# Spread modulation, eight plain blocks, and low parts of weights added by a GpSimd-queue DMA

## The chip, the core and the metric

The kernel runs on one core of a Trainium2 chip. A core has engines that each work through their own instructions in order: TensorE (PE; its weight loads are listed as PEld), VectorE (DVE), ScalarE (ACT), GpSimd (POOL) and SyncE (SP), which here only issues DMAs. Sixteen DMA engines move data between HBM and the on-chip SBUF; the queues of SP, ACT and POOL feed the same sixteen. The metric is the device time of one execution in microseconds (us), as the median of several runs.

## The reference

Two layers of a diffusion transformer over 256 latent tokens and 256 context tokens, model width 1024, float32. Layer 0 mixes with a short convolution, layer 1 with attention (8 query heads, 2 key/value heads, width 128). Around each mixer stand two feed-forward networks (FFNs). Cut to what matters here:

```python
for i in range(DEPTH):                                   # 2
    mod  = (silu(c) @ mod_w[i] + mod_b[i])               # 9 vectors of 1024: shift, scale, gate x 3
    modc = (silu(c_ctx) @ mod_w[i] + mod_b[i])
    lat = lat + 0.5 * gate * swiglu(modulate(lat, norm_g, shift, scale), w13, w2)
    cx  = cx  + 0.5 * gate * swiglu(modulate(cx, ...), w13, w2)
    lat, cx = mixer(...)                                 # conv in layer 0, attention in layer 1
    lat = lat + 0.5 * gate * swiglu(...)                 # second FFN; cx too in layer 0
# swiglu(h) = (silu(h @ w_gate) * (h @ w_up)) @ w2, hidden width 2816 = 22 blocks of 128
# modulate(t) = rms_norm(t) * g * (1 + scale) + shift
```

## The kernel before

Activations lie transposed: 128 features on the partitions, 512 tokens in the free dimension (256 latent, then 256 context), in 8 such tiles. Matmuls run in the fp32r type, and to keep float32 accuracy each operand is split in a high part (`hi`, rounded to fp32r by a ScalarE copy) and a low part (`lo = x - hi`, by VectorE): `split` (L89 to L92). `mm3` (L111 to L117) then issues three matmuls per product: high by high (L115), high weights by low activations (L116), low weights by high activations (L117).

Weights come in 1 MB tiles on the SP queue (`load_raw`, L85 to L87; tag `wr`, three buffers) and are split by half tiles of 128 x 1024 (tags `wh` and `wl`, four buffers each).

An FFN (`ffn`, l and b for layer and place) works in thirds of 8, 7 and 7 hidden blocks. Each third first makes its hidden blocks from `w13`, then `project` multiplies them by its part of `w2` into the 8 output tiles (`py`), and `finish` (L417) adds them to the residual `x` with the gate.

A hidden block over 512 tokens is made in one of two ways. The plain way (`w13_mm`, `w13_post`) takes 8 x 2 x 3 = 48 matmuls of 512 columns. The `Pair` way multiplies the 2 x 2 block matrix of gate and up weights with the 2 x 2 block matrix of the two token halves by a scheme with seven products in place of eight: 7 x 4 x 3 = 84 matmuls of 256 columns. It needs sums of the weights (S1 to S4, made by VectorE at L519, L525, L527 and then split) and sums of the activations (T1 to T4, made once per FFN by `sums`). The blocks A11, A12 and A22 are raw weights: A11 and A12 share one half tile of 128 x 1024 (`wh`, `wl`), A22 has its own of 128 x 512 (`w4h`, `w4l`, two buffers). In TensorE's order a Pair begins with its head, A11 into `p` and A12 into `q` (24 matmuls), then S1; the previous Pair's S3; S2 and S4; the previous Pair's A22. All FFNs but the last, which has 256 tokens, use Pairs; FFN (0,0) has three plain blocks at its start, FFNs (0,1) and (1,0) one, in the middle of which two Pairs' heads are issued.

Modulation is done by VectorE beside the matmuls: `mod_job` loads 1 MB of transposed `mod_w` and reduces 128 rows of 1024 at a time against silu(c) (L138), two row tiles by two streams, so four reductions in a row. `tick(share)` is called after an output tile, a convolution tile and so on, and starts a job when the shares add up to one; `mod_ready` runs whatever is still owed at once when a scale, shift or gate is needed. All of it is done before the attention.

The order on each engine is made when the kernel is built: a planner goes through the program by priority and readiness, gives each tile a free buffer of its tag, and writes the waits. An instruction that writes into a reused buffer waits for that buffer's last reader.

`Blocks.block` (L268 to L285) makes the normalised activations for Pairs: ScalarE writes them in float32, and for the first block a split follows after every second tile of 256 columns.

Of the kernel before, what the change touches and what calls it, by code (L numbers as in the profile page):

```python
# [9 lines left out]
F32 = mybir.dt.float32  # L10
# [6 lines left out]
P = 128  # L17
# [3 lines left out]
T2 = 2 * S  # L21
NM = 22
THIRDS = (8, 7, 7)
HEADS = 8
KVH = 2
EPS = 1e-6
# [11 lines left out]
def hybrid_kernel(ctx: ExitStack, tc: tile.TileContext, a: dict, out: bass.AP):  # L38
# [9 lines left out]
    modctx = ExitStack()  # L48
    mp = modctx.enter_context(tc.tile_pool(name="mp", bufs=2))

    uid = [0]

    def nm(s):
        uid[0] += 1
        return f"{s}{uid[0]}"
# [34 lines left out]
    def split(hi, lo, src):  # L90
        nc.scalar.activation(out=hi, in_=src, func=AF.Copy)  # L91
        nc.vector.tensor_tensor(out=lo, in0=src, in1=hi.bitcast(F32), op=ALU.subtract)  # L92
# [30 lines left out]
    def mod_tile(l, ch):  # L123
# [2 lines left out]
            done[l, ch] = 0  # L126
        return modv[l, ch]

    def mod_job(l, ch, pair):
        mt = mod_tile(l, ch)  # L130
        nv = 1 if (l == 1 and ch >= 5) else 2
        raw = load_raw(a["modT"][l, ch * 4 + pair])
        for j in range(2):
            kt = pair * 2 + j
            col = ch * KT + kt
            for v in range(nv):
                junk = mp.tile([P, D], BF16, name=nm("junk"), tag="junk", bufs=1)
                nc.vector.tensor_tensor_reduce(  # L138
                    out=junk,
                    in0=raw[:, j * D : j * D + D],  # L140
                    in1=scbc[:, v, :],
                    scale=1.0,
                    scalar=modb[:, l, col : col + 1],
                    op0=ALU.mult,
                    op1=ALU.add,
                    accum_out=mt[:, kt, v : v + 1],
                )
        done[l, ch] += 1

    jobs = [(0, ch, p) for ch in range(2, 9) for p in range(4)]  # L150
    jobs += [(1, ch, p) for ch in range(9) for p in range(4)]
    owed = [0.0]

    def tick(share):

        owed[0] += share
        while jobs and owed[0] >= 1:
            owed[0] -= 1
            mod_job(*jobs.pop(0))

    def mod_ready(l, ch):
        while not ((l, ch) in done and done[l, ch] == 4):
            mod_job(*jobs.pop(0))
        return modv[l, ch]

    def scale_of(l, j):
# [98 lines left out]
    class Blocks:  # L265
# [5 lines left out]
        def block(self, s, hf, A, B, ri, fine=False):  # L271
            raw = self.raw[hf, s] = hot("hr", F32)
            hi, lo = self.t["B", hf, s] = hot("bh"), hot("bl")
            for i in range(4):
                k = 4 * hf + i
                c = slice(i * S, i * S + S)
                t = scaled(s, k, A, ri)
                nc.scalar.activation(
                    out=raw[:, c], in_=t, func=AF.Identity, bias=B[:, k, s : s + 1]
                )  # L280
                if fine and i % 2:
                    c = slice((i - 1) * S, (i + 1) * S)
                    split(hi[:, c], lo[:, c], raw[:, c])
            if not fine:
                split(hi, lo, raw)  # L285

# [146 lines left out]
    def project(ws, src, nk, gate, tail, tot, late, ev, between=()):  # L433

        def products(ps, w, ks, c0, c1):  # L440
            for k in ks:
                mm3(ps[:, : c1 - c0], w(k), src(k, c0, c1), k == 0, k == nk - 1)

        nf = 3 if between else 2
        w2 = [ws(m) for m in range(nf)]
        p2 = [psum("py") for _ in range(nf)]
        cut = nk - 2 if between else nk - 1
        for i in range(nf):
            products(p2[i], w2[i], range(cut), 0, tot)
            if i < len(between):  # L450
                between[i]()
        if between:
            for i in range(nf):
                products(p2[i], w2[i], (nk - 2,), 0, tot)
        for i in range(nf):
            products(p2[i], w2[i], (nk - 1,), 0, tot)
            finish(i, p2[i], 0, tot, gate, tail)
            tick(ev)

        for m in range(nf, KT - late):  # L460
            if tail and tot == S and m == KT - 2:
                ready()
            w = ws(m)
            ps = psum("py")
            products(ps, w, range(nk), 0, tot)
            finish(m, ps, 0, tot, gate, tail)
            tick(ev)
        if late:

            wl = [ws(m) for m in (6, 7)]  # L470
# [25 lines left out]
    class Pair:  # L496
# [6 lines left out]
        def __init__(self, src, h):  # L503
# [5 lines left out]
            s1, s2, s3, s4 = (sm[:, i * T2 : i * T2 + T2] for i in range(4))  # L509
            self.w = {}  # L510

            def keep(keys, src):
                hi, lo = half()
                split(hi, lo, src)
# [56 lines left out]
    def ffn(l, b, h, tot, gate, tail, gs=(), ev=0.5):  # L571
        gs = list(gs)
        i0 = 0
        for t, n in enumerate(THIRDS):
            between = ()
            if tot == T2:
# [12 lines left out]
                    w13_post(pp, gs[0], 0, T2)  # L589
                prev = None  # L590
                for i in range(len(gs), n):
                    if heads:
# [14 lines left out]
                    gs.append(new_pair("g"))  # L607
                    prev.four(gs[-1])

                between = (prev.seven, last)  # L610
            else:
                for i in range(n):
                    w = load_w(a["w13"][l, b, i0 + i])
                    gs.append(new_pair("g"))
                    pp = psum("pg"), psum("pu")
                    w13_mm(pp, w, h, range(KT), 0, tot)
                    w13_post(pp, gs[i], 0, tot)
            i0 += n
            box = {}

# [122 lines left out]
    }  # L743
    for step in FIRST_STEPS.split():
        steps[step[0]](*(int(c) for c in step[1:]))
    done[0, 0] = done[0, 1] = 4
    h = FirstBlocks(h, h32)
    h.sums()
    for i in range(3):
        gs0.append(new_pair("g"))  # L750
        w13_post(pps[i], gs0[i], 0, T2)
# [13 lines left out]
    for m in range(KT):  # L765
# [36 lines left out]
        tick(1.2)  # L802

    def by_pairs(key):
        box = {}
# [9 lines left out]
    hn = Blocks()  # L815
    project(
        by_pairs("cw_out"), lambda k, c0, c1: (zs[k][0][:, c0:c1], zs[k][1][:, c0:c1]), KT,
        lazy_gate(0, 1), tail_norm(0, 2, hn), T2, 2, 0.5,
    )
    h = hn  # L820
    hn = Blocks()
    ffn(0, 1, h, T2, lazy_gate(0, 2), tail_norm(1, 0, hn), ())
    h = hn


    hn = Plain()
    ffn(1, 0, h, T2, lazy_gate(1, 0), tail_norm(1, 1, hn), (), 0.9)
    h = hn
    mod_ready(1, 8)
    modctx.close()  # L830
    ap = ctx.enter_context(tc.tile_pool(name="ap", bufs=2))


# [8 lines left out]
                start=True, stop=True,  # L842
            )

    def rotate(ps, gain, n, tag):

        kn = ap.tile([P, T2], F32, name=nm("kn"), tag=tag)
# [27 lines left out]

    def q_rope(p, ps):
        sums(ps, 4 * p)
        qr = rotate(ps, qg, 2, "qn")
        qs.append(new_pair("q"))
        split(qs[p][0], qs[p][1], qr)  # L880

# [5 lines left out]

    def k_rope(kv, ps):
        sums(ps, 16 + 4 * kv)
        krs.append(rotate(ps, kg, 1, "kn"))  # L890

    vs = []
    vt = []
# [42 lines left out]
    q_rope(0, pq[0])  # L936
    wk = load_w(a["wk"])
    pk = [k_proj(0)]
    q_rope(1, pq[1])
    pk.append(k_proj(1))  # L940
    k_rope(0, pk[0])
    pq.append(q_proj(2))
    k_rope(1, pk[1])
    inv_rms(16, 24)
    pq.append(q_proj(3))
# [75 lines left out]
    for hd in range(HEADS):  # L1021
        if hd + 2 < HEADS:
            pns[hd + 2] = scores(hd + 2)
        pts[hd] = turn(pns.pop(hd))
        if hd:
            mix(hd - 1, pts.pop(hd - 1))
    mix(HEADS - 1, pts.pop(HEADS - 1))


    hn = Plain(S)  # L1030
    project(
        by_pairs("wo"), lambda k, c0, c1: aos[k], KT, lazy_gate(1, 1), tail_norm(1, 2, hn), S, 0, 0,
    )
    ffn(
        1, 1, hn, S, lazy_gate(1, 2),
# [81 lines left out]
```

## Time and profile before

| | |
|---|---|
| median of 3 runs | 1635.89 us (1634.96 to 1641.69) |
| profiled execution | 1636.17 us, its span 1634.1 us, granted TensorE clock 0.984 |
| busy PE, DVE, ACT, POOL | 1581.4, 1358.5, 735.1, 0.2 us |
| DMA | 248.81 MB, 152 GB/s in the mean |

How rows are read. A group of instructions: line, engine, operation, out<-in by the program's names, shape, xcount | busy us, mean ns of one | idle time before them and what ended it. A wait: who <- whom, then us in total, times, longest us. A row in order of time: start in us from the span's beginning, duration in us, instruction, and in brackets the engine's idle time before it with what ended it. A row by stage: the stretch, its length, then for each engine busy us and instructions, the mean granted clock, the share of time that the DMA engines were busy, GB/s. A DMA row: what, queue, count, KB each, median us from issue to landing. Matmuls are pipelined, so a matmul's duration is longer than the distance to the next one's start.

### The profile page before, as it was taken

The page shows a single profiled execution, that of the slowest core. Times are in us where ns is not written, and L with a number is a line of the kernel's source. Part 1 is how long each engine was busy: PE and PEld are TensorE (multiplying, and loading weights), DVE is VectorE, ACT ScalarE, POOL GpSimd, SP SyncE. Part 2 cuts the span into 40 slices and gives each one's busy share as a digit, 9 for nine tenths or more (in the row PEclk, how much of TensorE's full clock was granted, in tenths as well). Part 3 has the DMA queues.
Part 4 walks back from the last instruction along what each step waited for, and adds up shares of the span by engine and source line. Part 5 has one row for each costly group of instructions (what it writes and reads, how often), then busy time and mean ns, then how long its engine had stood idle before and what let it go on. Part 6 is the DMA issues. An engine that isn't in the chain of part 4 may idle for free.

```text
span 1634.1 us, 26052 instructions
## 1 busy us (share of the span) xinstructions
PE 1581.4 (97%) x10746; PEld 1463.5 (90%) x10746; DVE 1358.5 (83%) x2066; ACT 735.1 (45%) x1131; POOL 0.2 (0%) x4
## 2 busy tenths in 40 slices
PE   9898999999999999999999999989999989999999
PEld 6697898998888889989899889789899879899999
DVE  4999998889988979898898989999898978756454
ACT  5552352554322356435245465235255346554443
POOL 0000000000000000000000000000000000000000
PEclk9999999999999999999999999999999989999999
DMA  8335525334445513452433513552633742245453
GB/s 317 132 106 189 195 98 189 114 124 174 150 171 187 188 52 104 155 180 97 163 141 116 182 52 109 185 197 97 247 136 126 270 172 94 78 146 190 168 186 112
DMA packets 38279, 248.81 MB, mean 152 GB/s; under 512 B 5136, under 2 KB 6928, under 8 KB 12304
## 3 DMA queue, kind: packets, MB, share of 16 engines
q1 hardware_dynamic: 35712, 245.38, 42.9%
q10 hardware_dynamic: 2448, 1.76, 0.4%
q8 instruction: 84, 1.38, 0.3%
q14 instruction: 35, 0.29, 0.0%
HBM read 244.77 MB, written 1.05 MB: 150 GB/s over the span
## 4 chain that ended last, share of the span: by engine, by line
PE 85%; DVE 10%; DMA 2%; ACT 1%; issue 1%; DVEq 0%; ACTq 0%; SPq 0%
PE py L115 8%; PE py L117 8%; PE py L116 8%; PE p L117 7%; PE p L115 7%; PE p L116 7%; PE q L117 5%; PE q L115 5%; PE q L116 5%; DVE junk L138 4%; DVE wl L92 2%; PE pg L116 2%; PE pg L115 2%; PE pg L117 2%; PE pu L116 2%; PE pu L117 2%
## 5 line engine op out<-in xcount | busy, mean ns | idle before, releaser
L91 ACT ACTIVATE wh<-wr 128x1024 fp32r<-128x1024 f32 (+2 forms) x269 | 269.9, 1013 | 401.6 <-PE py L116 92.2
L92 DVE TENSOR_TENSOR wl<-wr,wh 128x1024 fp32r<-128x1024 f32 (+2 forms) x269 | 311.5, 1165 | 103.0 <-ACT wh L91 102.4
L138 DVE CUSTOM_DVE_ANT_0 junk<-wr,scbc,modb 128x1024 bf16<-128x1024 f32 x236 | 302.4, 1281 | 28.1 <-DMA wr<-in_modT 25.4
L117 PE MATMUL py<-gh,wl 128*128 128x512 f32 (+1 forms) x746 | 264.0, 355 | 5.9 <-DVE wl L92 5.9
L115 PE MATMUL py<-gh,wh 128*128 128x512 f32 (+1 forms) x746 | 265.2, 355 | 4.6 <-ACT wh L91 4.6
L116 PE MATMUL py<-gl,wh 128*128 128x512 f32 (+1 forms) x746 | 265.1, 355 | 0.0
L92 DVE TENSOR_TENSOR wl<-ws,wh 128x1024 fp32r<-128x1024 f32 x122 | 148.7, 1223 | 30.0 <-ACT wh L91 29.7
L117 PEld LDWEIGHTS py<-gh,wl 128*128 128x128 f32 x746 | 142.0, 190 | 26.7 <-DVE wl L92 7.3
L91 ACT ACTIVATE wh<-ws 128x1024 fp32r<-128x1024 f32 x122 | 128.3, 1058 | 81.9 <-PE p L116 37.6
L115 PEld LDWEIGHTS py<-gh,wh 128*128 128x128 f32 x746 | 142.3, 191 | 24.1 <-ACT wh L91 5.7
L116 PEld LDWEIGHTS py<-gl,wh 128*128 128x128 f32 x746 | 142.2, 191 | 18.3
L116 PE MATMUL p<-tl,wh 128*128 128x256 f32 x488 | 138.2, 283 | 0.0
L115 PE MATMUL p<-th,wh 128*128 128x256 f32 x488 | 138.2, 283 | 0.0
L117 PE MATMUL p<-th,wl 128*128 128x256 f32 x488 | 137.8, 283 | 0.0
L115 PE MATMUL q<-bh,wh 128*128 128x256 f32 x336 | 95.2, 283 | 0.4 <-ACT gm L551 0.4
L116 PE MATMUL q<-bl,wh 128*128 128x256 f32 x336 | 95.2, 283 | 0.0
L117 PE MATMUL q<-bh,wl 128*128 128x256 f32 x336 | 95.1, 283 | 0.0
L116 PEld LDWEIGHTS p<-tl,wh 128*128 128x128 f32 x488 | 93.8, 192 | 0.3
L115 PEld LDWEIGHTS p<-th,wh 128*128 128x128 f32 x488 | 93.8, 192 | 0.3
L117 PEld LDWEIGHTS p<-th,wl 128*128 128x128 f32 x488 | 93.5, 192 | 0.0
L417 DVE SCALAR_TENSOR_TENSOR x<-py,G,x 128x256 f32<-128x256 f32 x168 | 73.6, 479 | 22.0 <-PE py L117 21.7
L91 ACT ACTIVATE gh<-gm 128x512 fp32r<-128x512 f32 (+1 forms) x88 | 50.7, 576 | 62.7 <-DVE gm L568 52.9
(234 smaller groups left out, 4073.5 us busy)
## 6 DMA issues: line engine op xcount, KB each, us to landing
wr<-in_w SPq DMA_DIRECT2D x88, 1024.0 KB, 4.9
wr<-in_modT SPq DMA_DIRECT2D x67, 1024.0 KB, 5.0
wr<-in_w2b SPq DMA_DIRECT2D x32, 896.0 KB, 4.6
wr<-in_w2a SPq DMA_DIRECT2D x16, 1024.0 KB, 4.8
wr<-in_cw_cx SPq DMA_DIRECT2D x8, 1024.0 KB, 4.9
wr<-in_mod SPq DMA_DIRECT2D x5, 1024.0 KB, 7.9
wr<-in_cw_b SPq DMA_DIRECT2D x4, 1024.0 KB, 4.9
wr<-in_cw_out SPq DMA_DIRECT2D x4, 1024.0 KB, 5.0
```

The lines of the kernel that those rows point to most:

```text
L91: nc.scalar.activation(out=hi, in_=src, func=AF.Copy)
L92: nc.vector.tensor_tensor(out=lo, in0=src, in1=hi.bitcast(F32), op=ALU.subtract)
L115: nc.tensor.matmul(ps, wh, mh, start=first, stop=False, **kw)
L116: nc.tensor.matmul(ps, wh, ml, start=False, stop=False, **kw)
L117: nc.tensor.matmul(ps, wl, mh, start=False, stop=last, **kw)
L138: nc.vector.tensor_tensor_reduce(out=junk, in0=raw[:, j * D : j * D + D], in1=scbc[:, v, :], scale=1.0, scalar=modb[:, l, col : col + 1], ...
L417: nc.vector.scalar_tensor_tensor(out=x[:, m, s * S : s * S + S], in0=ps[:, o : o + S], scalar=g[:, m, s : s + 1], in1=x[:, m, s * S : s * ...
```

## The change

Four things are changed together.

- Modulation is dealt out by single reductions (`mod_unit`, `next_unit`), not by jobs of four. `tick` counts in reductions, with new rates: 1.5 to 1.7 per output tile, 6 per convolution tile (4.8 before), 3 per plain block of the first FFN, and new calls in the attention (1, 1, 2, and 2 per head), in its output projection (1 per tile) and in the last FFN. What is owed is no longer finished before the attention, so the tiles of the modulation pool stay allocated, and `rotate` takes its tile from another pool.
- FFN (0,0) makes blocks 3 to 7 of its first third the plain way too (`AS_IS`), so that eight blocks are plain; `sums` is called after block 3.
- `project` asks for its weight tiles up to three output tiles ahead (`get`). For the first normalised block, `Blocks.block` makes the high part straight from the scaled tile, 256 columns at a time, and VectorE makes the low part from the same tile; the float32 copy comes after.
- In each of the 56 remaining Pairs the low parts of (A11, A12) and A22 are made by `split_by_dma`: ScalarE writes the high part, ScalarE writes its negative into the low tile, and a DMA on the GpSimd queue adds the weights from HBM onto it. That is 112 such DMAs, of 512 KB and 256 KB.

```diff
+AS_IS = {(0, 0): range(3, 8), (0, 1): (), (1, 0): ()}
...
+    def split_by_dma(hi, lo, src, dram):
+
+        nc.scalar.activation(out=hi, in_=src, func=AF.Copy)
+        nc.scalar.activation(out=lo, in_=hi.bitcast(F32), func=AF.Copy, scale=-1.0)
+        nc.gpsimd.dma_start(out=lo, in_=dram, accum_op=ALU.add)
...
+    def next_unit():
+        if not units:
+            l, ch, pair = jobs.pop(0)
+            mod_tile(l, ch)
+            raw = load_raw(a["modT"][l, ch * 4 + pair])
+            units.extend(
+                (l, ch, pair, raw, j, v) for j in range(2) for v in range(streams(l, ch))
+            )
+        mod_unit(*units.pop(0))
...
+                b = B[:, k, s : s + 1]
+                if fine:
+                    nc.scalar.activation(out=hi[:, c], in_=t, func=AF.Identity, bias=b)
+                    nc.vector.scalar_tensor_tensor(
+                        out=lo[:, c], in0=t, scalar=b, in1=hi[:, c].bitcast(F32),
+                        op0=ALU.add, op1=ALU.subtract,
+                    )
+                nc.scalar.activation(out=raw[:, c], in_=t, func=AF.Identity, bias=b)
...
+        def get(m):
+            for i in range(m, min(m + 3, KT)):
+                if i not in ahead:
+                    ahead[i] = ws(i)
+            return ahead[m]
...
-            keep(("A11", "A12"), raw[:, 1024:])
+            keep(("A11", "A12"), raw[:, 1024:], src[:, 1024:])
...
-            split(*self.w["A22"], a22)
+            split_by_dma(*self.w["A22"], a22, src[:, T2:1024])
...
+                    if t == 0 and not heads and i in AS_IS[l, b]:
+                        w = load_w(a["w13"][l, b, i])
+                        pp = psum("pg"), psum("pu")
+                        ...
+                        w13_mm(pp, w, h, range(4, KT), 0, T2)
+                        gs.append(new_pair("g"))
+                        w13_post(pp, gs[-1], 0, T2)
+                        if "T1" not in h.t:
+                            h.sums()
+                        else:
+                            tick(3)
+                        continue
```

More of the change, by code (lines that the diff above doesn't have):

```diff
@@ L47, in hybrid_kernel @@
     pss = ctx.enter_context(tc.tile_pool(name="pss", bufs=2, space=bass.MemoryType.PSUM))
-    modctx = ExitStack()
-    mp = modctx.enter_context(tc.tile_pool(name="mp", bufs=2))
+    mp = ctx.enter_context(tc.tile_pool(name="mp", bufs=2))
     uid = [0]
@@ L127, in mod_tile, with mod_unit @@
         return modv[l, ch]
+    def mod_unit(l, ch, pair, raw, j, v):
+        mt = mod_tile(l, ch)
+        kt = pair * 2 + j
+        col = ch * KT + kt
+        junk = mp.tile([P, D], BF16, name=nm("junk"), tag="junk", bufs=1)
+        nc.vector.tensor_tensor_reduce(
+            out=junk,
+            in0=raw[:, j * D : j * D + D],
+            in1=scbc[:, v, :],
+            scale=1.0,
+            scalar=modb[:, l, col : col + 1],
+            op0=ALU.mult,
+            op1=ALU.add,
+            accum_out=mt[:, kt, v : v + 1],
+        )
+        done[l, ch] += 1
@@ L129, in mod_job, with streams @@
+    def streams(l, ch):
+        return 1 if l == 1 and ch >= 5 else 2
     def mod_job(l, ch, pair):
-        mt = mod_tile(l, ch)
-        nv = 1 if (l == 1 and ch >= 5) else 2
+        mod_tile(l, ch)
         raw = load_raw(a["modT"][l, ch * 4 + pair])
         for j in range(2):
[L134 to L147, printed above, removed]
@@ L148, in mod_job @@
-        done[l, ch] += 1
+            for v in range(streams(l, ch)):
+                mod_unit(l, ch, pair, raw, j, v)
     jobs = [(0, ch, p) for ch in range(2, 9) for p in range(4)]
     jobs += [(1, ch, p) for ch in range(9) for p in range(4)]
+    units = []
     owed = [0.0]
-    def tick(share):
-        owed[0] += share
-        while jobs and owed[0] >= 1:
+    def next_unit():
+        if not units:
+            l, ch, pair = jobs.pop(0)
+            mod_tile(l, ch)
+            raw = load_raw(a["modT"][l, ch * 4 + pair])
[3 more added lines that the diff above has]
+        mod_unit(*units.pop(0))
@@ L158, in tick @@
+    def tick(n):
+        owed[0] += n
+        while (jobs or units) and owed[0] >= 1:
             owed[0] -= 1
-            mod_job(*jobs.pop(0))
+            next_unit()
     def mod_ready(l, ch):
-        while not ((l, ch) in done and done[l, ch] == 4):
-            mod_job(*jobs.pop(0))
+        while not ((l, ch) in done and done[l, ch] == 8 * streams(l, ch)):
+            next_unit()
         return modv[l, ch]
@@ L277, in block @@
                 t = scaled(s, k, A, ri)
[L278 to L283, printed above, removed]
+                b = B[:, k, s : s + 1]
[4 more added lines that the diff above has]
+                        op0=ALU.add, op1=ALU.subtract,
+                    )
+                nc.scalar.activation(out=raw[:, c], in_=t, func=AF.Identity, bias=b)
             if not fine:
@@ L444, in project @@
         nf = 3 if between else 2
-        w2 = [ws(m) for m in range(nf)]
+        ahead = {}
+        def get(m):
[3 more added lines that the diff above has]
+            return ahead[m]
+        w2 = [get(m) for m in range(nf)]
         p2 = [psum("py") for _ in range(nf)]
@@ L462, in project @@
                 ready()
-            w = ws(m)
+            w = get(m)
             ps = psum("py")
@@ L468, in project @@
         if late:
-            wl = [ws(m) for m in (6, 7)]
+            wl = [get(m) for m in (6, 7)]
             if tail:
@@ L510, in __init__, with keep @@
             self.w = {}
-            def keep(keys, src):
+            def keep(keys, part, dram=None):
                 hi, lo = half()
-                split(hi, lo, src)
+                if dram is None:
+                    split(hi, lo, part)
+                else:
+                    split_by_dma(hi, lo, part, dram)
                 for i, key in enumerate(keys):
                     self.w[key] = [t[:, i * T2 : i * T2 + T2] for t in (hi, lo)]
-            keep(("A11", "A12"), raw[:, 1024:])
+            keep(("A11", "A12"), raw[:, 1024:], src[:, 1024:])
             tt(
@@ L569, in four, with ffn @@
             split(g[0], g[1], self.gm)
-    def ffn(l, b, h, tot, gate, tail, gs=(), ev=0.5):
+    def ffn(l, b, h, tot, gate, tail, gs=(), ev=1.5):
         gs = list(gs)
@@ L617, in ffn @@
                     w13_post(pp, gs[i], 0, tot)
+                    tick(1)
             i0 += n
@@ L745, in hybrid_kernel @@
         steps[step[0]](*(int(c) for c in step[1:]))
-    done[0, 0] = done[0, 1] = 4
+    done[0, 0] = done[0, 1] = 16
     h = FirstBlocks(h, h32)
-    h.sums()
     for i in range(3):
@@ L801, in hybrid_kernel @@
         split(zs[m][0], zs[m][1], z)
-        tick(1.2)
+        tick(6)
     def by_pairs(key):
@@ L843, in sums, with rotate @@
             )
-    def rotate(ps, gain, n, tag):
-        kn = ap.tile([P, T2], F32, name=nm("kn"), tag=tag)
+    def rotate(ps, gain, n):
+        kn = hot("kn", F32)[:, :T2]
         nc.scalar.activation(out=kn, in_=ps, func=AF.Identity, scale=gain)
@@ L938, in hybrid_kernel @@
     pk = [k_proj(0)]
+    tick(1)
     q_rope(1, pq[1])
     pk.append(k_proj(1))
+    tick(1)
     k_rope(0, pk[0])
     pq.append(q_proj(2))
+    tick(2)
     k_rope(1, pk[1])
@@ L1026, in hybrid_kernel @@
             mix(hd - 1, pts.pop(hd - 1))
+        tick(2)
     mix(HEADS - 1, pts.pop(HEADS - 1))
```

24 lines of the change are left out of this document (15 added, 9 removed).

## The prediction

> **What bounds the kernel now.** I read the page's first parts, then the stages, TensorE's own waits, and one stretch in order of time. On the page TensorE is nearly always busy, VectorE comes second, GpSimd is idle.
>
> ```profile
> span 1634.1 us, 26052 instructions
> PE 1581.4 (97%) x10746; PEld 1463.5 (90%) x10746; DVE 1358.5 (83%) x2066; ACT 735.1 (45%) x1131; POOL 0.2 (0%) x4
> PE 85%; DVE 10%; DMA 2%; ACT 1%; issue 1%; DVEq 0%; ACTq 0%; SPq 0%
> ```
>
> Busy time by stage, with the granted clock:
>
> ```profile
> core 0: us, PE busy (x) PEld busy (x) DVE busy (x) ACT busy (x) POOL busy (x), PEclk, DMA share, GB/s
> 0.00:100.00 100.00, 89.92 (x488) 70.81 (x489) 74.38 (x141) 53.74 (x100) 0.20 (x4) 0.95 0.58 205
> 100.00:200.00 100.00, 91.90 (x563) 81.88 (x562) 93.92 (x139) 33.80 (x49) 0.00 (x0) 0.95 0.50 173
> 200.00:400.00 200.00, 200.00 (x1407) 188.41 (x1406) 178.52 (x256) 93.60 (x139) 0.00 (x0) 1.00 0.40 141
> 560.00:640.00 80.00, 76.18 (x560) 72.81 (x559) 67.80 (x97) 47.08 (x76) 0.00 (x0) 0.98 0.25 83
> 920.00:1000.00 80.00, 76.00 (x574) 72.96 (x573) 72.40 (x103) 50.03 (x81) 0.00 (x0) 0.98 0.30 106
> 1000.00:1120.00 120.00, 112.27 (x742) 102.88 (x741) 113.62 (x164) 45.63 (x66) 0.00 (x0) 0.99 0.48 167
> 1280.00:1340.00 60.00, 51.44 (x299) 46.85 (x299) 53.45 (x103) 26.39 (x45) 0.00 (x0) 0.89 0.57 206
> 1340.00:1440.00 100.00, 93.09 (x692) 86.97 (x692) 73.90 (x156) 57.39 (x108) 0.00 (x0) 0.99 0.31 103
> ```
>
> The long Pair stretches (200 to 400) lose nothing: 200.00 of 200.00 busy at clock 1.00, so there no relief of another engine can pay. Losses sit where VectorE is late. TensorE's waits name it:
>
> ```profile
> PE p L117 <- DVE wl L92: 8.6, 3, 5.0
> PE pg L115 <- ACT bh L91: 6.1, 2, 3.0
> PE py L117 <- DVE wl L92: 5.9, 2, 3.5
> PE py L115 <- ACT wh L91: 4.6, 1, 4.6
> ```
>
> **Plain blocks for five Pairs: +3.6 us.** TensorE's price is its pitch, the distance of starts:
>
> ```profile
> 314.47 0.28 PE L115 MATMUL p<-hh,wh 128*128 128x256 f32 x1
> 314.59 0.28 PE L116 MATMUL p<-hl,wh 128*128 128x256 f32 x1
> 314.71 0.28 PE L117 MATMUL p<-hh,wl 128*128 128x256 f32 x1
> ...
> 435.81 0.39 PE L115 MATMUL pc<-hh,wh 128*128 128x512 f32 x1
> 436.04 0.39 PE L116 MATMUL pc<-hl,wh 128*128 128x512 f32 x1
> 436.26 0.39 PE L117 MATMUL pc<-hh,wl 128*128 128x512 f32 x1
> ```
>
> That is 0.120 us at 256 columns and 0.225 at 512. A Pair is 84 x 0.120 = 10.1 us, a plain block 48 x 0.225 = 10.8; five swaps cost 5 x 0.72 = 3.6.
>
> **Modulation by units, new tick rates, finer normalisation: -27 us.** Durations:
>
> ```profile
> L138 DVE CUSTOM_DVE_ANT_0 junk<-wr,scbc,modb 128x1024 bf16<-128x1024 f32 x236 | 302.4, 1281 | 28.1 <-DMA wr<-in_modT 25.4
> L92 DVE TENSOR_TENSOR wl<-wr,wh 128x1024 fp32r<-128x1024 f32 x193 | 235.2, 1221 | 80.1 <-ACT wh L91 79.6
> L92 DVE TENSOR_TENSOR w4l<-wr,w4h 128x512 fp32r<-128x512 f32 x61 | 41.8, 685 | 0.0
> ```
>
> All 236 products stay. A job of four blocks VectorE for 4 x 1.28 = 5.1 us, and the first gate forced four jobs at once (20 us). By stage, idle time of the table plus (1 - clock) x stretch: 0 to 100 has the 5.0 us wait for `wl` behind the sums ahead of the first Pair; with plain blocks there, -5. 100 to 200: 8.1 idle and up to 5 of clock, the forced burst; -11. 560 to 640 and 920 to 1000: 3.8 and 4.0 idle; the first high block now comes after one 256-column step, not after a pair and a 512-column split; -2 each. 1000 to 1120: 7.7; the new rates leave the built order with a burst of ten units at that first gate, so half, -4. 1280 to 1340: 8.6 idle and 6.6 clock; half, -8. 1340 to 1440: 20 units move into the attention, 20 x 1.28 = 26 us onto a VectorE that has 26 us free there: +5, bounds 0 and +15. Sum -27, bounds -40 and -8. Weight prefetch three ahead and raw buffers held longer by spread units: 0, since a 1 MB load (4.9 us, below) serves 10 us of matmuls; without that cover a late load costs its remainder.
>
> **Low parts by DMA.** 56 Pairs remain. VectorE loses 56 x (1.22 + 0.69) = 107 us, all in stretches without loss: gain 0. ScalarE gains 56 x (1.06 + 0.63) = 95 us, on 735: no bound. What counts is the lateness of `wl` of (A11, A12). A stretch of one Pair, ScalarE and then VectorE in order of time:
>
> ```profile
> 307.35 1.06 ACT L91 ACTIVATE wh<-wr 128x1024 fp32r<-128x1024 f32 x1 [0.42 <-PE q L116]
> 308.91 0.37 ACT L551 COPY gm<-q 128x256 f32<-128x256 f32 x1 [0.50 <-PE q L117]
> 314.55 0.63 ACT L91 ACTIVATE w4h<-wr 128x512 fp32r<-128x512 f32 x1 [1.56 <-PE p L116]
> 317.43 1.06 ACT L91 ACTIVATE wh<-wr 128x1024 fp32r<-128x1024 f32 x1 [0.42 <-PE q L116]
> ...
> 308.54 1.22 DVE L92 TENSOR_TENSOR wl<-wr,wh 128x1024 fp32r<-128x1024 f32 x1
> 310.35 0.43 DVE L562 TENSOR_TENSOR p<-p,gm 128x256 f32<-128x256 f32 x1 [0.60 <-PE p L117]
> ```
>
> The period is 317.43 - 307.35 = 10.08 us. ScalarE can start the high part only when the previous head's `q` products free the buffer; VectorE has the low part at 309.76; its first reader starts at 314.71, so 4.9 us are spare. After the change: high part to 308.41, its negative 1.06 more, about 309.5; the GpSimd queue issues the 512 KB accumulate; it must land by about 314.5. So the DMA has X* = 5.0 us from issue to landing, and each Pair is late by X - 5.0. The `gm` copy queued behind the negative then ends at 309.9, and VectorE's reader of it starts at 310.35: nothing. The 256 KB accumulate for A22 has 19 us by the built order, and it stands on the GpSimd queue some 3 us ahead of the next Pair's 512 KB (it follows the `w4h` step, near 316): nothing. SP's loads keep their number. In the built order 40 of the 56 (A11, A12) buffers have this window (62 matmuls, 7.4 us); in the FFNs (0,1) and (1,0), which form two heads inside their first block, the second head has 30 matmuls, 3.6 us, twice (X* = 1.2), and one first head 5.5 us (X* = 3.1); the rest have slack.
>
> X is not in this trace: no GpSimd DMA, no accumulate. Nearest rows, median us to landing:
>
> ```profile
> wr<-in_w SPq DMA_DIRECT2D x88, 1024.0 KB, 4.9
> wr<-in_w2b SPq DMA_DIRECT2D x32, 896.0 KB, 4.6
> wr<-in_wk SPq DMA_DIRECT2D x1, 1024.0 KB, 7.0
> scbc<-in_c SPq DMA_DIRECT2D x2, 512.0 KB, 8.1
> rt<-kn ACTq DMA_DIRECT2D x8, 32.0 KB, 1.9
> ```
>
> 128 KB more cost 0.3 us, so a plain 512 KB load is an estimated 3.7: the low end. The high end is 8.1, the slowest 512 KB row (beside other loads). An accumulate needs the weights and what stands in the tile, 1 MB to be read, so 4.9 is nearest; a queue of which no row tells, and the raw load and the A22 accumulate that share the engines, push toward the crowded 7.0. I take the middle, 6.0.
>
> The Trainium skill says the reading side counts: in Collectives: The Full Stack, The bandwidth ceiling, a reduce sends two source descriptors per chunk down one ring and runs at half a copy's rate. No run so far shows it. Against my lateness stands DMA: Bandwidth & Descriptors, Anatomy of one DMA: a GpSimd-queue DMA takes about 2.0 us plus bytes at 436 GB/s, an estimated 3.2 us for 512 KB, or 4.4 with both reads; by that rule every window of 7.4 us holds and the sum is the first rival's. For 1 MB it gives 4.4 where the row here has 4.9.
>
> Cost at X = 6.0: 40 x 1.0 = 40, 2 x 4.8 = 9.6, 2.9 for the first head: +53. At 3.7: 2 x 2.5 + 0.6 = 6. At 8.1: 40 x 3.1 + 2 x 6.9 + 5 = 143.
>
> **Sum** against the profiled execution (1636.17 us, of it a span of 1634.1; the runs' median is 1635.89, so it is typical): 1636.2 + 3.6 - 27 + 53 = 1666 us.
>
> **Rivals.** First, the accumulate lands within its window (X up to 5.0, say 4.5): 2 x 3.3 + 1.4 = 8 remains, 1636.2 + 3.6 - 27 + 8 = 1621, faster. For it: 32 KB takes 1.9, and 1 MB 4.9, just inside. Against it: the unmeasured queue and company on the engines. It decides at X = 5.4, where 40 x 0.4 + 2 x 4.2 + 2.3 = 27 eats what the spreading gives. Second, the accumulate is far slower, X = 8.5, by slow issue or slow adding: 40 x 3.5 + 2 x 7.3 + 5.4 = 160, so 1773. For it: nothing rated it here. Against: the loads are only 0.40 of the DMA engines' time in the Pair stretch. Third, the DMA hides but the attention takes the 26 us of moved units badly and the bursts stay (-8 in place of -27): 1636.2 + 3.6 - 8 + 8 = 1640, no change.
>
> **Chances.** Lateness as forecast (X of 5.4 to 7.5) 0.47; first rival 0.28; second 0.17; third 0.08. Within 0.5% (8 us, about what a measurement can tell from no change) falls the third rival, plus 0.02 of X near 5.4: faster 0.28, same 0.10, slower 0.62. Range: from 1605 (X inside, -40 in place of -27) to 1760 (X = 8.1); the likeliest case's own is 1640 to 1730. Both tails together leave out about 2 in 10.
>
> **What would show it.** Right: in the Pair stretches TensorE waits once per Pair in the third matmul of the split (`p<-..,wl`) for the DMA into `wl`, about 1 us, and the period of the ScalarE `wh<-wr` starts is 11.1, not 10.08; accumulates land in about 6.0; the 5.0 us wait and the burst before 165 are gone; VectorE is near 1225 us, ScalarE near 815. Wrong: a landing below 5 us and a period of 10.08; or landings far over 7; or waits of TensorE in the attention that outgrow the rest.

## The result and the profile after

The changed kernel takes 1730.88 us (1727.97 to 1738.73, four runs) beside 1635.85 us (1634.96 to 1641.69) of the kernel before, measured beside it: a ratio of 1.058, 95% interval 1.054 to 1.062. It is slower, as forecast, but by 95 us and not by 30. The profiled execution took 1729.46 us, its span 1727.7.

The first part of the page of the changed kernel, and its chain of waits:

```profile
span 1727.7 us, 25954 instructions
PE 1610.3 (93%) x10566; PEld 1474.4 (85%) x10566; DVE 1245.6 (72%) x1923; ACT 808.9 (47%) x1222; POOL 98.0 (6%) x116
PE 49%; issue 30%; DMA 9%; DVE 6%; POOL 3%; ACT 2%; POOLq 0%; ACTq 0%; SPq 0%; DVEq 0%
```

TensorE was busy 97% of the span before and is busy 93% now, VectorE falls from 83% to 72%: work was taken off the engine that was not the bound. In the chain, "issue" is time in which an engine waited for nothing that the profile shows. What TensorE waits for is mostly one thing. The first row of TensorE's waits (us in total, times, longest):

```profile
PE p L124 <- DMA wl<-in_w: 82.5, 51, 6.1
```

The row of the kernel before that stood here, `p` for `wl` by VectorE (8.6 us), is gone; in its place 51 of the 56 Pairs wait for the DMA. The same stages as before (the same times, not quite the same work):

```profile
100.00:200.00 100.00, 97.40 (x524) 84.52 (x523) 69.05 (x100) 37.07 (x48) 6.22 (x7) 1.00 0.58 179
200.00:400.00 200.00, 188.12 (x1275) 174.51 (x1274) 139.01 (x202) 99.00 (x145) 18.34 (x21) 0.99 0.61 163
640.00:920.00 280.00, 255.37 (x1744) 238.15 (x1744) 189.43 (x262) 137.44 (x199) 28.75 (x33) 0.98 0.63 168
1000.00:1120.00 120.00, 106.33 (x741) 100.99 (x740) 79.69 (x103) 64.63 (x96) 10.44 (x12) 0.93 0.51 127
1280.00:1340.00 60.00, 53.05 (x414) 52.03 (x413) 34.29 (x42) 34.84 (x53) 6.99 (x9) 0.94 0.65 154
```

100 to 200, with the forced burst before, is nearly full now. But 200 to 400, which lost nothing, now loses 12 us, and 640 to 920 loses 25.

A steady Pair in order of time (start, duration, and in brackets the idle time before with what ended it), the high part, its negative, the issue on GpSimd's queue, and TensorE's first reader of the low part:

```profile
304.51 1.06 ACT L97 ACTIVATE wh<-wr 128x1024 fp32r<-128x1024 f32 x1 [0.95 <-PE q L123]
305.60 1.06 ACT L98 ACTIVATE wl<-wh 128x1024 fp32r<-128x1024 f32 x1
...
307.06 0.89 POOL L99 DMA_DIRECT2D wl<-in_w  x1 [12.09 <-ACT gm L589]
...
312.57 0.38 PE L124 MATMUL p<-hh,wl 128*128 128x256 f32 x1 [0.54 <-DMA wl<-in_w]
...
349.44 1.06 ACT L97 ACTIVATE wh<-wr 128x1024 fp32r<-128x1024 f32 x1 [0.42 <-PE q L123]
```

Four Pairs lie between the two high parts at 304.51 and 349.44: a period of 11.23 us, where it was 10.08 and 11.1 was forecast. The negative ends at 306.66, 0.40 us later the DMA is issued, and TensorE has the low part at 312.57.

The DMA queues of the changed kernel (packets, MB, share of sixteen engines' span) and the DMAs (KB each, median us from issue to landing):

```profile
q1 hardware_dynamic: 35712, 245.38, 40.7%
q0 software_dynamic: 16128, 44.05, 15.8%
...
wl<-in_w POOLq DMA_DIRECT2D x56, 512.0 KB, 6.0
w4l<-in_w POOLq DMA_DIRECT2D x56, 256.0 KB, 5.1
```

So the unknown of the prediction, X, came out at the 6.0 us that was taken for it, and yet the sum was 65 us short.

### The profile page after: what moved, and what is told of

Read it like the earlier page. It is cut to its first block, busy times and chain, and to the rows that moved or that the text cites. A ratio compares the mean times of both kernels' runs of the same rounds, so it can differ in the third digit from the quotient of the medians.

```text
span 1727.7 us, 25954 instructions
## 1 busy us (share of the span) xinstructions
PE 1610.3 (93%) x10566; PEld 1474.4 (85%) x10566; DVE 1245.6 (72%) x1923; ACT 808.9 (47%) x1222; POOL 98.0 (6%) x116
## 3 DMA queue, kind: packets, MB, share of 16 engines
q0 software_dynamic: 16128, 44.05, 15.8%
HBM read 288.81 MB, written 1.05 MB: 168 GB/s over the span
## 4 chain that ended last, share of the span: by engine, by line
PE 49%; issue 30%; DMA 9%; DVE 6%; POOL 3%; ACT 2%; POOLq 0%; ACTq 0%; SPq 0%; DVEq 0%
DMA wl<-in_w 8%; PE py L122 7%; PE py L123 7%; PE py L124 7%; PE pg L123 2%; PE pg L122 2%; PE pg L124 2%; PE pu L123 2%; PE pu L124 2%; PE pu L122 2%; POOL w4l L99 2%; DVE junk L142 2%; POOL wl L99 2%; PE p L124 1%; PE p L123 1%
## 5 line engine op out<-in xcount | busy, mean ns | idle before, releaser
L92 ACT ACTIVATE wh<-wr 128x1024 fp32r<-128x1024 f32 (+2 forms) x218 | 214.9, 1002 | 319.5 <-PE py L123 97.2
L93 DVE TENSOR_TENSOR wl<-wr,wh 128x1024 fp32r<-128x1024 f32 (+2 forms) x218 | 249.8, 1153 | 110.5 <-ACT wh L92 110.1
L93 DVE TENSOR_TENSOR wl<-ws,wh 128x1024 fp32r<-128x1024 f32 x112 | 137.1, 1225 | 49.2 <-ACT wh L92 49.2
L123 PE MATMUL p<-tl,wh 128*128 128x256 f32 x448 | 127.0, 283 | 1.6 <-DVE tl L93 1.6
L122 PE MATMUL p<-th,wh 128*128 128x256 f32 x448 | 126.8, 283 | 0.6 <-ACT th L92 0.6
L124 PE MATMUL p<-th,wl 128*128 128x256 f32 x448 | 126.8, 283 | 0.0
L600 DVE TENSOR_TENSOR p<-p,gm 128x256 f32<-128x256 f32 x56 | 24.2, 432 | 135.8 <-PE p L124 135.8
L124 PE MATMUL p<-bh,wl 128*128 128x256 f32 x168 | 56.1, 334 | 68.1 <-DMA wl<-in_w 68.0
L124 PEld LDWEIGHTS p<-bh,wl 128*128 128x128 f32 x168 | 35.9, 214 | 76.2 <-DMA wl<-in_w 76.2
L97 ACT ACTIVATE wh<-wr 128x1024 fp32r<-128x1024 f32 x56 | 59.3, 1059 | 87.3 <-DMA wr<-in_w 43.0
```

The source lines that it names most:

```text
L122: nc.tensor.matmul(ps, wh, mh, start=first, stop=False, **kw)
L123: nc.tensor.matmul(ps, wh, ml, start=False, stop=False, **kw)
L124: nc.tensor.matmul(ps, wl, mh, start=False, stop=last, **kw)
L600: nc.vector.tensor_tensor(out=self.u[:, S:], in0=self.p, in1=self.gm[:, S:], op=ALU.add)
```

## The experiments

**All low parts by VectorE again.** First question: is the whole loss the DMA's, or do the other parts cost something too?

```diff
-            keep(("A11", "A12"), raw[:, 1024:], src[:, 1024:])
+            keep(("A11", "A12"), raw[:, 1024:])
...
-            split_by_dma(*self.w["A22"], a22, src[:, T2:1024])
+            split(*self.w["A22"], a22)
```

> The changed kernel, but VectorE makes all low parts again (no low part by DMA); spread modulation, plain blocks, prefetch and finer normalisation stay. Theory (the loss is TensorE's waits for low parts, and the clock that falls behind them): the 91.0 us of waits on the DMA into wl go, and with them about 22 us of lost clock and slow restarts: 1729 - 91 - 22 = 1616 us, between 1605 and 1640, faster than before. Rival (the spreading, the plain blocks or the moved reductions themselves cost time, so that the waits on DMA only took the place of other waits): 1640 to 1660, no gain over before.

1614.44 us, a ratio to the kernel before of 0.987 (0.984 to 0.989). Its page:

```profile
span 1613.8 us, 25613 instructions
PE 1580.1 (98%) x10566; PEld 1452.6 (90%) x10566; DVE 1332.3 (83%) x2035; ACT 722.8 (45%) x1110; POOL 0.2 (0%) x4
```

Its stages 200 to 400 and 1280 to 1340:

```profile
200.00:400.00 200.00, 199.80 (x1399) 187.60 (x1399) 170.20 (x256) 92.46 (x140) 0.00 (x0) 1.00 0.38 132
1280.00:1340.00 60.00, 59.61 (x444) 56.34 (x444) 51.88 (x97) 31.55 (x56) 0.00 (x0) 1.00 0.53 184
```

VectorE is as busy as before (83%) and TensorE is at 98%. The rest of the change gains 20.3 us of span (1634.1 - 1613.8); the low parts by DMA cost 1727.7 - 1613.8 = 113.9. No run here is clearly faster.

**The DMA alone, in the kernel before.** Are the long waits a matter of the spread reductions and the prefetch?

```diff
-            keep(("A11", "A12"), raw[:, 1024:])
+            keep(("A11", "A12"), raw[:, 1024:], src[:, 1024:])
...
-            split(*self.w["A22"], a22)
+            split_by_dma(*self.w["A22"], a22, src[:, T2:1024])
```

> The kernel before, with nothing changed but the low parts of raw blocks by DMA, in all its 61 Pairs; modulation in jobs of four, no plain blocks added, no prefetch. Theory (the accumulate is late by itself, most of all at the start of a third, whatever surrounds it): steady Pairs 45 x 1.1 = 50, second heads 2 x 4.8 = 10, starts of thirds 8 x 4.5 = 36, minus nothing regained, clock +10: 1636 + 105 = about 1735 to 1745 us. Rival (the starts of thirds are late only since spread reductions and prefetch tie the raw buffers and crowd the loads): steady Pairs and second heads alone, 1636 + 60 = about 1690 to 1700 us.

1753.88 us, ratio 1.072 (1.069 to 1.074). TensorE's first wait:

```profile
PE p L123 <- DMA wl<-in_w: 97.2, 56, 9.1
```

The cost comes without the rest of the change, and the longest wait, 9.1 us, is longer than any in the changed kernel. The rival is out; the theory was 9 us too low even at its upper end (1745 us).

**Which of the two accumulates.** One kernel adds only A22 by DMA, the other only (A11, A12).

```diff
# A22 alone
-            keep(("A11", "A12"), raw[:, 1024:], src[:, 1024:])
+            keep(("A11", "A12"), raw[:, 1024:])
# (A11, A12) alone
-            split_by_dma(*self.w["A22"], a22, src[:, T2:1024])
+            split(*self.w["A22"], a22)
```

> The changed kernel with only A22's low part (256 KB) by DMA; A11 and A12 have theirs by VectorE. Theory (A22 has 19 us of slack): no wait on w4l, the time that the kernel without any low part by DMA has, within 5 us (about 1616). Rival (56 more DMAs of 256 KB crowd the raw weight loads, and those are what is late at the starts of thirds): some 20 us more than without them, about 1636.

> The changed kernel with only (A11, A12)'s low part (512 KB) by DMA; A22 has its by VectorE. Theory (steady Pairs keep their 1.1 us, the starts of thirds lose the company of the A22 accumulates only in part): 1715 to 1729 us. Rival (the A22 accumulates are the crowd that makes the 512 KB ones late at the starts of thirds): the waits there fall from 6 us to 1, about 1690 us.

A22 alone: 1616.76 us, 0.988 (0.985 to 0.990), not to be told from 0.987 without any DMA. (A11, A12) alone: 1723.38 us, 1.053 (1.050 to 1.055). The busy times and the DMA row of A22 alone, then TensorE's first wait of (A11, A12) alone:

```profile
PE 1579.9 (98%) x10566; PEld 1451.6 (90%) x10566; DVE 1304.4 (81%) x1979; ACT 751.0 (47%) x1166; POOL 49.1 (3%) x60
...
w4l<-in_w POOLq DMA_DIRECT2D x56, 256.0 KB, 4.9
```

```profile
PE p L124 <- DMA wl<-in_w: 80.6, 50, 5.8
```

56 accumulates with slack are free, though they take 28 us off VectorE (1332.3 to 1304.4) and give nothing back either. The other 56 carry nearly all of the loss, without the first ones for company. Their slow landings stay too: at the second Pairs of the later thirds four of them still take 8.3 to 10.5 us (one at 867.5 us of this run 10.5), so that does not need the A22 accumulates for company.

**The queue, or the adding?** The same DMA, as a plain copy: nothing is subtracted, and the low parts hold the whole weights.

```diff
-        nc.gpsimd.dma_start(out=lo, in_=dram, accum_op=ALU.add)
+        nc.gpsimd.dma_start(out=lo, in_=dram)
```

> The changed kernel, but the GpSimd-queue DMA copies the weights over the negative in place of adding them, so the subtraction is left out and the low parts hold the weights themselves; same queue, same bytes from HBM, same places. Theory (the adding is what costs: in the changed kernel's table of DMA queues 44.05 MB took 15.8% of 1727.7 us, 6.2 us of all sixteen engines per MB, where the SP loads of before took 42.9% of 1634.1 us for 245.38 MB, 2.9 us per MB): the queue's share falls to about 7.5%, the 512 KB land in about 4.3 us, steady Pairs stop waiting, second heads wait 3 us, and the kernel takes about 1630 to 1650 us. Rival (the GpSimd queue and its issue cost it, whatever the DMA does): landing stays at 6 us and the time at 1715 to 1730.

1644.61 us, 1.005 (1.003 to 1.007). Queue and landing:

```profile
q0 software_dynamic: 16128, 44.05, 9.2%
...
wl<-in_w POOLq DMA_DIRECT2D x56, 512.0 KB, 4.0
w4l<-in_w POOLq DMA_DIRECT2D x56, 256.0 KB, 4.1
```

and TensorE's wait for it:

```profile
PE p L124 <- DMA wl<-in_w: 18.7, 9, 3.7
```

With the same bytes from HBM on the same queue, landing falls from 6.0 to 4.0, and 51 waits become 9. The time that the queue's packets took on the sixteen engines goes from 15.8% x 1727.7 = 273 us to 9.2% x 1642.8 = 151, or from 6.2 to 3.4 us per MB: adding costs 1.8 times a copy. So 86 of the loss of 116 us (1730.88 - 1614.44) come with the adding. The other 30 (1644.61 - 1614.44) stay without it; what the queue, the issue, the negative and the company of the loads each have in them was not separated.

**Two pieces.** Half as much to add before A11 can be read.

```diff
-                    split_by_dma(hi, lo, part, dram)
+                    for d in (slice(0, T2), slice(T2, 1024)):
+                        split_by_dma(hi[:, d], lo[:, d], part[:, d], dram[:, d])
```

> The changed kernel with the (A11, A12) low part in two pieces of 128 x 512, each with its own high part, negative and 256 KB accumulate, A11 first. Theory (a piece costs about 1.6 us of the sixteen engines and about 3 us fixed): A11's negative ends 0.9 us earlier and its 256 KB land in about 5 rather than 6, so A11 is there 1.9 us earlier and the 1.1 us waits of the steady Pairs go; A12 is read 1.4 us after A11 and is just in time; second heads and starts of thirds gain 1 to 2 us each: 1729 - 46 - 15 - some clock = about 1660. Rival (one more 0.9 us issue and a second fixed cost on the same queue put A12 behind): the waits move from p to q and the time stays at 1715 to 1735.

1668.63 us, 1.021 (1.018 to 1.025). Queue and landing:

```profile
q0 software_dynamic: 24192, 44.05, 16.8%
...
wl<-in_w POOLq DMA_DIRECT2D x112, 256.0 KB, 5.4
```

and TensorE's waits for it, in the first and in the second head product:

```profile
PE p L124 <- DMA wl<-in_w: 28.2, 12, 4.8
...
PE q L124 <- DMA wl<-in_w: 3.6, 2, 1.8
```

The engines' time for the adding is the same (16.8% of a span of 1664.0 us, 280 us), but the 5.4 us mix the two pieces: the first, A11's, lands in 4.8 us in the median, the second in 5.8, where the whole took 6.0. A11's piece is also issued 0.5 us earlier, and not the 0.9 that were expected (2.1 us behind the start of the high part, where it was 2.55 at 304.51). Together that is more than the 1.1 us of a steady Pair. Twelve waits are left, of 2.4 us in the mean, and `q` hardly waits. The time came 9 us above the theory and far below the rival.

**The starts of the thirds by VectorE.** Two Pairs in each second and third third, 12 of 56; the new last argument of `Pair` is `early`.

```diff
-                        pr = Pair(a["w13"][l, b, i0 + i], h)
+                        pr = Pair(a["w13"][l, b, i0 + i], h, t > 0 and i < 2)
...
-            keep(("A11", "A12"), raw[:, 1024:], src[:, 1024:])
+            keep(("A11", "A12"), raw[:, 1024:], None if early else src[:, 1024:])
...
-            split_by_dma(*self.w["A22"], a22, src[:, T2:1024])
+            if early:
+                split(*self.w["A22"], a22)
+            else:
+                split_by_dma(*self.w["A22"], a22, src[:, T2:1024])
```

> The changed kernel, but VectorE makes the low parts of the first two Pairs in the second and third thirds of each FFN (12 of the 56 Pairs). Theory (the starts of thirds are a cost of their own, 30.5 us of waits in 12 Pairs in the changed kernel, since the accumulate meets two or three weight loads there, and the clock falls behind the long ones): the 30.5 us go and some 6 us of clock with them: about 1690. Rival (every Pair costs the same X minus its window, and the starts only show waits that come anyway): 12 x 1.1 us, about 1715. A second rival (the crowd moves to the third Pair of each third): about 1710, with waits of 3 us or more at the third Pair.

1697.38 us, 1.038 (1.034 to 1.041), and TensorE's first wait:

```profile
PE p L124 <- DMA wl<-in_w: 54.9, 44, 4.6
```

27.6 us of waits gone with 12 Pairs, and 32.6 us of span (1727.7 - 1695.1), where 12 times 1.1 would be 13. The starts are a cost of their own. The crowd moved on in two places (waits of about 4.2 us come new at 755.5 and 1150.5), so the second rival has a small part.

What happens there is seen in the changed kernel, in a Pair that is the second of a third. In order of time, ScalarE, GpSimd and TensorE:

```profile
742.09 1.06 ACT L97 ACTIVATE wh<-wr 128x1024 fp32r<-128x1024 f32 x1 [0.52 <-PE py L123]
744.59 0.37 ACT L583 COPY sg<-p 128x256 f32<-128x256 f32 x1 [1.44 <-PE p L124]
744.86 1.07 ACT L98 ACTIVATE wl<-wh 128x1024 fp32r<-128x1024 f32 x1
...
746.32 0.88 POOL L99 DMA_DIRECT2D wl<-in_w  x1 [4.45 <-ACT wl L98]
...
756.66 0.58 PE L124 MATMUL p<-bh,wl 128*128 128x256 f32 x1 [6.11 <-DMA wl<-in_w]
```

the DMAs issued from 736 to 760:

```profile
wr<-in_w SPq DMA_DIRECT2D x3, 1024.0 KB, 9.6
wl<-in_w POOLq DMA_DIRECT2D x2, 512.0 KB, 8.1
w4l<-in_w POOLq DMA_DIRECT2D x2, 256.0 KB, 9.8
```

and the stage before the end of the wait, and the one around it:

```profile
748.00:754.00 6.00, 2.55 (x22) 2.34 (x20) 4.89 (x6) 2.13 (x3) 0.00 (x0) 1.00 1.05 321
754.00:761.00 7.00, 4.34 (x20) 4.34 (x21) 0.68 (x1) 0.90 (x2) 0.00 (x0) 0.53 0.17 65
```

Four accumulates and three 1 MB loads are issued within some 10 us (737.04 to 747.42), the DMA engines are full (1.05), and this accumulate needs about 10.3 us from issue, not 6.0; the loads too take 9.6 us in the median and not 5.0. Besides, the negative stood on ScalarE's queue behind a copy that waited for `p`, and started 1.7 us late. And in the 7 us around the end of the wait, 754 to 761, the granted clock is 0.53.

**Without the added plain blocks**, and **with modulation in jobs of four** (no low part by DMA in either): where does the gain of 20 us come from?

```diff
# without plain blocks
-AS_IS = {(0, 0): range(3, 8), (0, 1): (), (1, 0): ()}
+AS_IS = {(0, 0): (), (0, 1): (), (1, 0): ()}
...
     h = FirstBlocks(h, h32)
+    h.sums()
# in jobs of four: tick and mod_ready as before the change, at its rates
-            next_unit()
+            mod_job(*jobs.pop(0))
...
+    mod_ready(1, 8)
```

> The kernel without any low part by DMA (VectorE makes them, 1614 us), and without the five added plain blocks: those are Pairs again, and the sums of the first FFN are made before its first Pair as before the change. Theory (the prediction's terms): -3.6 us of TensorE's pitch, +5 for the wait behind the sums: 1616, and not further than 5 us from 1614. Rival (the plain blocks free VectorE early, so that the modulation is on time at the first gate, and that is most of the gain): 1622 to 1640.

> The kernel without any low part by DMA (1614 us), with modulation in jobs of four at the rates of before and finished before the attention; plain blocks, prefetch and finer normalisation stay. Theory (the prediction's terms: the burst at the first gate, the one in 1000 to 1120 and the one in 1280 to 1340 come back, -5 for what moved into the attention): 1614 + 11 + 4 + 8 - 5 = about 1632. Rival (the gain is from the plain blocks and the finer normalisation): 1615 to 1620.

Without plain blocks: 1627.77 us, 0.996 (0.994 to 0.997). In jobs of four: 1644.23 us, 1.005 (1.003 to 1.006). TensorE's first wait without plain blocks, and the stages 100 to 200 and 1280 to 1340 with jobs of four:

```profile
PE p L124 <- DVE wl L93: 8.0, 2, 5.0
```

```profile
100.00:200.00 100.00, 95.25 (x462) 80.90 (x461) 81.00 (x120) 25.69 (x34) 0.00 (x0) 0.95 0.48 169
1280.00:1340.00 60.00, 48.30 (x281) 43.39 (x280) 56.92 (x113) 25.91 (x43) 0.00 (x0) 0.86 0.64 225
```

The 5.0 us wait behind the sums is back without plain blocks; the bursts are back with jobs of four (1280 to 1340: 11.7 us idle and a clock of 0.86). Both theories missed, by 12 us each; without plain blocks the rival's range came, and with jobs of four neither. Without plain blocks the loss lies in the first 200 us: TensorE is busy 89.81 and 92.45 us of the first two hundreds there, and 95.13 and 100.00 with them. One part alone gains some 8 us, the other alone loses as much, both together gain 21, so they aren't a sum. A likely reason, not shown, is that the plain blocks make room on VectorE in the first FFN and single reductions fill it; the run in jobs of four also leaves out the calls of `tick` in the plain blocks, so size and places weren't told apart.

**Prefetch and the finer first block**, each undone in the kernel without low parts by DMA:

```diff
# prefetch
-            for i in range(m, min(m + 3, KT)):
+            for i in range(m, m + 1):
# first block: float32 copy first, as before the change
-                if fine:
-                    nc.scalar.activation(out=hi[:, c], in_=t, func=AF.Identity, bias=b)
...
+                if fine and i % 2:
+                    c = slice((i - 1) * S, (i + 1) * S)
+                    split(hi[:, c], lo[:, c], raw[:, c])
```

> The kernel without any low part by DMA (1614 us), with the weight tiles of the output projections asked for one at a time, as before the change, and not three ahead. Theory (the prediction put prefetch at nothing, since loads of 4.9 us serve 10 us of matmuls): 1614, within 4 us. Rival (with modulation spread in between, a late load or a late split shows as soon as it is not asked for early): 1620 to 1635.

> The kernel without any low part by DMA (1614 us), with the first normalised block made as before the change (float32 copy first, a split after every second tile). Theory (the prediction gave the finer normalisation 2 us at each of the two places where an FFN starts): 1614 + 4 = 1618. Rival (TensorE waits there for the norm itself, not for the split): 1614, within 1.5 us.

Without prefetch 1615.27 us, 0.988 (0.986 to 0.990); with the old first block 1617.23 us, 0.989 (0.987 to 0.991); with both parts in place it was 0.987 (0.984 to 0.989). No worth of prefetch is to be seen, as forecast. The finer block may be worth the 4 us that were forecast, but that is within what the intervals leave open.

## Why the prediction fell short

**Direction and mechanism of a steady Pair: right.** TensorE is the bound, relief of VectorE pays nothing, and the DMA is late by X minus its window. The likeliest case (X from 5.4 to 7.5) is the one that came, but with a time at the upper edge of its own range (1640 to 1730).

**Plain blocks and modulation, +3.6 - 27 = -23.4: right as a sum,** measured at -20.3 (span without low parts by DMA), but partly by luck. The split into parts was not right: taking the plain blocks out cost 13 us and not the 1.4 of +3.6 and -5, and taking the spreading out some 30 and not 18; they act on each other, and the prediction added them.

**Low parts by DMA, +53: this is the step that failed.** Measured at +113.9. Term by term, from the distances of TensorE's starts in the profiled execution (the waits so measured sum to 90.7 us; the view of waits, which leaves small ones out, has 82.5):

| term | forecast | measured |
|---|---|---|
| steady Pairs | 40 x 1.0 = 40 | 39 waits, 43.7 |
| second heads | 2 x 4.8 = 9.6 | 4.6 + 4.9 = 9.5 |
| first heads | 2.9 | 1.2 + 4.3 = 5.5 |
| starts of thirds ("the rest have slack") | 0 | 8 waits, 32.0 |
| clock after long waits | 0 | about 17 |
| remainder, not taken apart | 0 | about 6 |

The first three were sized well, from a price that no row had shown: 6.0 was the middle of two bounds, and that it came so close is luck. So, in part, are the second heads: their windows were 4.7 and 5.7 us and not 3.6, but the negative stood 0.9 and 1.8 us behind other work of ScalarE.

The fourth is the sentence "the rest have slack". It was read from the built order, with one X for all, and it is wrong in two ways. First, six of these Pairs, the second of each later third, have hardly more room than a steady one. The kernel before shows it, in the high part and the first reader of the low part at such a place:

```profile
297.23 1.06 ACT L91 ACTIVATE wh<-wr 128x1024 fp32r<-128x1024 f32 x1 [0.80 <-PE py L116]
...
304.63 0.28 PE L117 MATMUL p<-hh,wl 128*128 128x256 f32 x1
```

That is 7.4 us, as in the steady Pair at 307.35 and 314.71; in the changed kernel the six have 6.4 to 8.3. All six wait, 25.1 us together. About 8 of them would come at an X of 6.0. The rest is X itself: at a third's start loads and accumulates come together, and X grows to between 7.5 and 10.8 us in five of the six. Second, the raw weights of a third's first Pair come late, so that its high part starts late. The group of the high parts of (A11, A12) in the changed kernel has this in five Pairs, 43.0 us of ScalarE's idle time; behind the second bar stands the idle time, with what ended it:

```profile
L97 ACT ACTIVATE wh<-wr 128x1024 fp32r<-128x1024 f32 x56 | 59.3, 1059 | 87.3 <-DMA wr<-in_w 43.0 <-PE q L123 21.8 <-PE py L123 13.7
```

Most of the first Pairs have room for that. One has not: its high part starts at 1144.76, 2.9 us ahead of the reader, and TensorE waits 6.1 us though X is 6.1; another waits 0.7. The loads are late without the DMA too, as the group that holds the high parts in the kernel with all low parts by VectorE shows:

```profile
L92 ACT ACTIVATE wh<-wr 128x1024 fp32r<-128x1024 f32 x198 | 208.1, 1058 | 308.2 <-PE pg L123 84.8 <-PE py L123 63.2 <-DMA wr<-in_w 48.1
```

There TensorE has no wait in `p` for a low part: VectorE's 1.2 us still fit behind the late load, a DMA of 6 us does not. That is why the DMA's crowding rows, which the prediction quoted for X (7.0 and 8.1 us), belonged to these Pairs, not to the range alone.

The fifth term was left out altogether. The mean granted clock fell from 0.984 to 0.974, where the kernel without DMA has 0.989. One minus the clock, times the span, is 44.9 us against 17.8; a part of that falls into waits, where it costs nothing, and by the distances of TensorE's starts at half clock an estimated 17 us of the difference are left. All eight waits of 4 us and more in the changed kernel, measured by these distances, have a stretch at half clock, 3.4 or 6.8 us long, around or just behind their end; the 754 to 761 row above is one. The Trainium skill has that rule in TensorE: Matmul & The Clock Gate, Part 1: The HAM clock gate: an idle window of about 3.4 us halves the clock until the array has been busy for one. The trace agrees in the lengths, the stretches being 3.4 us or twice that; but waits of 2.0 and 3.0 us (ending at 606.9 and 1012.9) were followed by half clock too, and there the measurement decides. By the lengths of the stretches a wait of 4 us or more is to be priced with 1.7 to 3.4 us on top, an estimate; with eight such waits that is 14 to 27 us.

**X, the time to land.** Adding took 6.2 us of the DMA engines per MB, copying 3.4, and 512 KB landed in 6.0 and 4.0 us. The first rival, which rested on landing inside 5 us, fell with the 6.0. The Trainium skill's rule that a reduce runs at half a copy's rate since it reads two sources (Collectives: The Full Stack, The bandwidth ceiling) comes near the measured 1.8; that the second read is the reason is not shown by a run here. The Trainium skill's formula in DMA: Bandwidth & Descriptors, Anatomy of one DMA, gave an estimated 3.2 us for a plain 512 KB and 4.4 with both reads, where 4.0 and 6.0 were measured; the measurement decides.

**The rivals.** The first (1621) would have needed the plain copy's 4.0 us, and even then the starts cost: the copy took 1644.61. The second (X of 8.5, 1773) has the X of the accumulates at the starts of thirds, in five Pairs (7.5 to 10.8) and not in 56. The third (spreading fails) is refuted by 1614.44.

**What would show it.** The period (11.1 forecast, 11.23), the wait in the third matmul, the landing (6.0), ScalarE (815 forecast, 808.9) and, 20 us off, VectorE (1225 forecast, 1245.6) came as named; so did the end of the 5.0 us wait and of the burst.

## What to carry to other kernels

Moving work off an engine that is not the bound pays nothing, and if the work comes back with a longer latency in front of the bound, the cost is latency minus window for each use, plus the places where the new transfers meet old ones. So price an added transfer not once but per place: read the window there from the trace, in us, and take the transfer's median where the DMA engines have room, and the crowded rows where the trace already shows late loads. Then add the clock: a stall that is long enough costs again after it has ended.

## What was not expected of the hardware

- An accumulate took 1.8 times the DMA engines' time of a plain copy on the same queue (6.2 and 3.4 us per MB of weights), and 2.0 us more to land for 512 KB (6.0 and 4.0).
- Half the size lands little sooner: plain copies of 512 and 256 KB took 4.0 and 4.1 us, accumulates 6.0 and 5.1 (4.8 for the first of two pieces).
- In a crowd everything slows together: an accumulate took 10.3 us and a 1 MB load 9.6 where three loads met four accumulates within some 10 us, and with (A11, A12) alone by DMA an accumulate among loads still took 10.5.
- Waits of TensorE of 4 us and more came with half clock each time, an estimated 17 us in all beyond the kernel without them.
